# Expanding router gates into a dense matrix: strided evacuations, one-hot blocks of four, and gate products on GpSimd

## The chip, the core and the metric

The kernel runs on one core of one Trainium2 chip. TensorE (PE), VectorE (DVE), ScalarE (ACT), GpSimd (POOL) and SyncE (SP, which here issues transfers) each have a queue of their own, worked off in order, and they wait for one another by semaphores. The metric is device time in microseconds (us) of one execution.

## The reference, cut to what matters

The program is one layer of a streaming encoder for 1152 tokens (1024 prompt, 128 sample tokens): two attention branches, a merge, a product-key mixture of 128 x 128 single-neuron experts (PEER), and a per-layer embedding. The change touches PEER only:

```python
q = (xi @ w_q).reshape(t, PEER_HEADS, 2, PEER_DK // 2)
s = jnp.einsum('thpc,hpnc->thpn', q, sub_keys).astype(jnp.float32)
top_s, top_i = lax.top_k(s, PEER_TOPK)
...
best_s, pos = lax.top_k(cand_s, PEER_TOPK)
idx = jnp.take_along_axis(cand_i, pos, axis=-1)
g = jax.nn.softmax(best_s, axis=-1)
hid = jax.nn.gelu(jnp.einsum('thkd,td->thk', u[idx], xi).astype(jnp.float32))
wgt = (g * hid).astype(xi.dtype)
return jnp.einsum('thk,thkd->td', wgt, v[idx])
```

Every token picks 16 experts in each of 8 heads, 128 in all. An expert has two indices i and j, each below 128 (idx = 128 i + j), and a gate g.

## The kernel before, in words

The nine tiles of 128 tokens are split. For four of them the rows of the chosen experts are gathered one by one (GpSimd indirect transfers, line 813, worked on by DVE in lines 816 and 818). For the five tiles in `DENSE` (640 tokens) all 16384 experts are computed, and a gate that is zero for experts that were not chosen picks out the right ones. Their weights come from a dense matrix G in DRAM, `G_d`, with 128 x 128 gates a token.

Three stages lie one behind the other here.

- `hidden_phase` computes the hidden rows of 36 of the 128 values of j ahead of time. It is planned with low priority, so that it fills gaps in whatever runs; its end reaches into the expansion. In `hidden` the rows of u are split in a high and a low part: `uh` on ACT (line 940) and `ul`, a subtraction, on POOL (line 941; on DVE for rows of the dense phase), then multiplied (line 958) and put through gelu on ACT (line 961).
- `expand_phase` builds G. For each tile, `prepare` turns the index and gate rows (i, j, g, each 128 slots x 128 tokens) so that the slots lie on the partitions: `rb` holds i and j as bf16, `gT` the gates. Then, for each block of W = 8 tokens: DVE compares `iota_i` with the i of each token and gets one-hot rows `oa` in bf16 (line 916), laid out with the eight tokens innermost, and compares `iota` with j to get `ob` in f32 (line 917, called obb in the profile). The product of `oa` with the gate is `ga`, in f32 with 128 contiguous values a token: in every second block (GD = 2) one DVE instruction for all eight tokens (line 919), in the others eight ACT instructions (line 923). Both read `oa` in steps of eight bf16, 16 bytes. PE multiplies ga and ob token by token (line 927) and so sums over the 128 slots: four tokens fill one PSUM bank `pg`. ACT copies a bank into `stage` (line 929). `stage` is [j, token] in SBUF, 64 tokens wide; the copy reads PSUM in order and writes single values in steps of 64 f32. When 64 tokens are there, SP writes `stage` to `G_d` (line 933).
- `dense_phase` then goes over j: it reads the gates of two values of j (line 979), multiplies them with the hidden row (line 987), splits the result, and PE multiplies it with the rows of v (lines 1009 to 1011). The rest of the gathers runs beside it.

Tiles of a pool with tag `oa`, `ga` or `obb` have two buffers each (`ex` has bufs = 2): a block takes over the buffer of the block before the last, when all that read it are done. `pg` comes in turns from two kinds of banks with two buffers each. Order: the order of each queue isn't written by hand. A planner simulates the program with its own model of what instructions cost, and by priorities fixes for each engine the order in which it works.

Of the kernel before, what the change touches and what calls it, by code (L numbers as in the profile page):

```python
# [10 lines left out]
BF = mybir.dt.bfloat16  # L11
# [3 lines left out]
OP = mybir.AluOpType  # L15
# [3 lines left out]
P = 128  # L19
# [16 lines left out]
GD = 2  # L36
# [10 lines left out]
def build(tc, I, O, dbg=None, stop=None):  # L47
    nc = tc.nc
    top = ExitStack()

    def pool(stack, name, bufs=1, **kw):
        return stack.enter_context(tc.tile_pool(name=name, bufs=bufs, reuse_waits="tile", **kw))
# [20 lines left out]
    def bank(name, w=512):  # L73
        return psb.tile([P, 512], F32, tag="b1", name=name)
# [810 lines left out]
    def expand_phase():  # L885

        st = ExitStack()
        ex = pool(st, "ex", 2)
        W = 8
        iota = ex.tile([P, W, P], BF, name="iota", bufs=1)  # L890
        nc.gpsimd.iota(iota, pattern=[[0, W], [1, P]], base=0, channel_multiplier=0, allow_small_or_imprecise_dtypes=True)
        iota_i = ex.tile([P, P, W], BF, name="iota_i", bufs=1)
        nc.gpsimd.iota(iota_i, pattern=[[1, P], [0, W]], base=0, channel_multiplier=0, allow_small_or_imprecise_dtypes=True)
        def prepare(t):
            src = ex.tile([P, 3, P], F32, tag="src", name=f"src{t}")
            nc.sync.dma_start(src, rt_d[t].rearrange("k p c -> p k c"))
            ps = bank(f"rT{t}")
            for k in range(3):
                nc.tensor.transpose(ps[:, k * P:(k + 1) * P], src[:, k, :], ident)
            rb = ex.tile([P, 2, P], BF, tag="rb", name=f"rb{t}")  # L900
            nc.scalar.copy(rb, ps[:, 0:2 * P].rearrange("p (k c) -> p k c", k=2))
            gT = ex.tile([P, P], F32, tag="gT", name=f"gT{t}")
            nc.scalar.copy(gT, ps[:, 2 * P:3 * P])
            return rb, gT

        ready = prepare(DT[0])
        for n, t in enumerate(DT):
            rb, gT = ready
            for c0 in range(0, P, W):
                if c0 % 64 == 0:  # L910
                    stage = ex.tile([P, P, 64], F32, tag="stage", name=f"stage{t}{c0}")
                cw = slice(c0, c0 + W)
                oa = ex.tile([P, P, W], BF, tag="oa", name=f"oa{t}_{c0}")
                ga = ex.tile([P, W, P], F32, tag="ga", name=f"ga{t}_{c0}")
                ob = ex.tile([P, W, P], F32, tag="obb", name=f"obb{t}_{c0}")
                nc.vector.tensor_tensor(oa, iota_i, rb[:, 0, cw].unsqueeze(1).broadcast_to([P, P, W]), op=OP.is_equal)
                nc.vector.tensor_tensor(ob, iota, rb[:, 1, cw].unsqueeze(2).broadcast_to([P, W, P]), op=OP.is_equal)
                if (c0 // W) % GD == 0:
                    nc.vector.tensor_tensor(ga, oa.rearrange("p i c -> p c i"),
                                            gT[:, cw].unsqueeze(2).broadcast_to([P, W, P]), op=OP.mult)  # L920
                else:
                    for c in range(W):
                        nc.scalar.mul(ga[:, c, :], oa[:, :, c], gT[:, c0 + c:c0 + c + 1])  # L923
                for b0 in range(0, W, 4):
                    pg = (bank if b0 % 8 == 0 else zbank)(f"pg{t}{c0}{b0}")
                    for c in range(4):
                        nc.tensor.matmul(pg[:, c * P:(c + 1) * P], ga[:, b0 + c, :], ob[:, b0 + c, :], start=True, stop=True)  # L927
                    o = (c0 + b0) % 64
                    nc.scalar.copy(stage[:, :, o:o + 4].rearrange("p j t -> p t j"), pg.rearrange("p (t j) -> p t j", t=4))
                if c0 == 64 and n + 1 < len(DT):  # L930
                    ready = prepare(DT[n + 1])
                if c0 % 64 == 64 - W:
                    nc.sync.dma_start(G_d[2 * n + c0 // 64], stage)
        st.close()
# [136 lines left out]
    if stop is None or stop == "full":  # L1071
        de = ExitStack()
        hs = ExitStack()
        hp = pool(hs, "hp", 2)
        r2s, res = route_phase(1, B, aT1)
        hidden_phase(hp, *aT1)
        r2s.close()
        expand_phase()
        dp = pool(de, "dp")
        yacc = [dp.tile([P, D], F32, name=f"yacc{t}") for t in DT]  # L1080
        dense_phase(hp, yacc, *aT1)
        gathers(9999)
        sg.close()
        ple_phase(hp, A, DT, yacc, aT1)
        de.close()
        hs.close()
# [104 lines left out]
```

## Time and profile before

| | |
|---|---|
| median of 3 runs (lowest to highest) | 4101.27 us (4084.70 to 4101.39) |
| the profiled execution: its own time | 4085.47 us |
| the span of its trace | 4083.8 us |
| granted TensorE clock in it, mean | 0.964 |
| start of the first oa to the end of the last copy of stage | 2010.8 to 2307.7 us of the span |
| instructions of the expansion: oa, obb, products on DVE | 80, 80, 40 |
| products on ACT, copies of stage on ACT | 320, 160 |

How to read it: a row of a group gives line, engine, operation, the tiles written and read, their shapes, how often, then the busy time, the mean time of one in ns, and the engine's idle time just before them with what ended it. A row of the order of time gives start, duration (both us), engine, line, operation, and in brackets the idle time before it. Instructions of one kind in a row are merged there (x8), and successive instructions of an engine overlap somewhat, so the distance from start to start says what one costs the engine. PE counts each f32 multiplication as two records.

### The profile page before, as it was taken

The numbers are of one execution on the slowest core, as the hardware profiler recorded it, in microseconds if no ns is written. First come the engines' busy times: TensorE is split into PE (matmuls) and PEld (weight loads), VectorE is DVE, ScalarE is ACT, GpSimd is POOL, SyncE is SP. The second block draws the span as 40 slices with busy tenths as digits, with TensorE's granted clock in tenths as the row PEclk, the third lists the DMA queues.
The fourth block names the chain that finished last, engine by engine and source line by source line (L and its number), as shares of the span: only waits on it lengthen the run. The fifth ranks groups of instructions, "written<-read, shape, count | busy, mean of one in ns | idle before, by whom it ended". The sixth has DMA issues, their size and how long they took to land.

```text
span 4083.8 us, 57125 instructions
## 1 busy us (share of the span) xinstructions
PE 3716.3 (91%) x20520; PEld 3048.3 (75%) x20520; DVE 2969.9 (73%) x5571; ACT 1539.4 (38%) x3307; POOL 1721.3 (42%) x1360
## 2 busy tenths in 40 slices
PE   7988899869889897899897899999999999999999
PEld 6555566657767565798886788888888888888876
DVE  5122112899888777799888588888888888888862
ACT  5445412346565411224599722222222222212231
POOL 5112032137767555652310044555555555555520
PEclk8999999879999898899999999999999999999999
DMA  6777733328888898972343589989988998988952
GB/s 206 237 235 208 223 93 124 101 82 268 281 288 275 286 321 294 328 247 88 108 184 165 230 297 314 325 309 315 325 304 304 313 331 316 327 298 311 313 173 71
DMA packets 415116, 1002.49 MB, mean 245 GB/s; under 512 B 38816, under 2 KB 170352, under 8 KB 412400
## 3 DMA queue, kind: packets, MB, share of 16 engines
q0 software_dynamic: 147456, 536.94, 38.0%
q1 hardware_dynamic: 267376, 461.90, 34.0%
q8 instruction: 161, 2.64, 0.3%
q14 instruction: 123, 1.01, 0.1%
HBM read 917.19 MB, written 81.50 MB: 245 GB/s over the span
## 4 chain that ended last, share of the span: by engine, by line
issue 25%; PE 22%; DMA 20%; DVE 19%; POOL 11%; ACT 3%; SPq 0%; POOLq 0%; DVEq 0%; ACTq 0%
DMA v<-in_pv,gi 9%; POOL u L813 6%; DMA u<-in_pu,gi 5%; POOL v L813 4%; DVE gya L818 3%; DVE u L816 3%; PE Sd L547 2%; DMA vs<-in_pv 1%; DMA vcd<-in_vA 1%; PE z L209 1%; PE pu L638 1%; PE hd L958 1%; PE po L497 1%; PE z L210 1%; PE z L211 1%
## 5 line engine op out<-in xcount | busy, mean ns | idle before, releaser
L813 POOL DMA_INDIRECT v<-in_pv,gi x512 | 669.5, 1308 | 794.0 <-DVE gya L818 654.9
L813 POOL DMA_INDIRECT u<-in_pu,gi x512 | 669.2, 1307 | 494.3 <-DVE u L816 374.4
L816 DVE SCALAR_TENSOR_TENSOR u<-u,gn 128x1024 f32<-128x1024 f32 x512 | 630.0, 1239 | 167.0 <-DMA u<-in_pu,gi 164.5
L818 DVE SCALAR_TENSOR_TENSOR gya<-v,hid,gya 128x1024 f32<-128x1024 f32 x512 | 661.1, 1291 | 121.3 <-DMA v<-in_pv,gi 117.4
L1009 PE MATMUL py<-vh,wh 128*128 128x512 f32 x1280 | 507.9, 398 | 46.4 <-DVE yacc L1012 23.0
L1011 PE MATMUL py<-vh,wl 128*128 128x512 f32 x1280 | 497.9, 394 | 6.4 <-DVE wl L941 6.4
L1010 PE MATMUL py<-vl,wh 128*128 128x512 f32 x1280 | 502.4, 394 | 0.2 <-DVE vl L941 0.2
L958 PE MATMUL hd<-aTh,uh 128*128 128x320 f32 x2048 | 483.4, 313 | 21.0 <-ACT gp L961 14.1
L958 PE MATMUL hd<-aTh,ul 128*128 128x320 f32 x2048 | 482.8, 313 | 7.0 <-DVE ul L941 5.7
L958 PE MATMUL hd<-aTl,uh 128*128 128x320 f32 x2048 | 482.0, 313 | 0.0
L958 PEld LDWEIGHTS hd<-aTh,uh 128*128 128x128 f32 x2048 | 351.8, 191 | 31.9 <-ACT gp L961 16.0
L958 PEld LDWEIGHTS hd<-aTh,ul 128*128 128x128 f32 x2048 | 349.9, 190 | 13.7 <-DVE ul L941 7.8
L958 PEld LDWEIGHTS hd<-aTl,uh 128*128 128x128 f32 x2048 | 351.1, 191 | 4.0
L940 ACT CAST vh<-vs 128x1024 fp32r<-128x1024 f32 x128 | 134.1, 1052 | 500.0 <-DMA vs<-in_pv 267.7
L1009 PEld LDWEIGHTS py<-vh,wh 128*128 128x128 f32 x1280 | 242.4, 190 | 106.9 <-DVE yacc L1012 29.4
L1011 PEld LDWEIGHTS py<-vh,wl 128*128 128x128 f32 x1280 | 242.4, 189 | 61.3 <-DVE wl L941 10.6
L1010 PEld LDWEIGHTS py<-vl,wh 128*128 128x128 f32 x1280 | 242.8, 190 | 47.5 <-DVE vl L941 0.4
L940 ACT CAST uh<-us 128x1024 fp32r<-128x1024 f32 x128 | 134.2, 1048 | 285.7 <-PE hd L958 266.7
L940 ACT CAST wh<-ge 128x640 fp32r<-128x640 f32 x128 | 91.9, 727 | 390.7 <-DVE ge L987 195.5
L927 PE MATMUL pg<-obb,ga 128*128 128x128 f32 x1280 | 192.5, 296 | 42.2 <-ACT ga L923 22.2
L927 PEld LDWEIGHTS pg<-obb,ga 128*128 128x128 f32 x1280 | 164.0, 195 | 70.5 <-ACT ga L923 28.8
L1012 DVE TENSOR_TENSOR yacc<-yacc,py 128x1024 f32<-128x1024 f32 x160 | 192.4, 1214 | 11.5 <-PE py L1011 11.5
(1051 smaller groups left out, 7368.7 us busy)
## 6 DMA issues: line engine op xcount, KB each, us to landing
us<-in_uT SPq DMA_DIRECT2D x128, 512.0 KB
vs<-in_pv SPq DMA_DIRECT2D x128, 512.0 KB
G_d<-stage SPq DMA_DIRECT2D x10, 4096.0 KB
gj<-G_d SPq DMA_DIRECT2D x64, 640.0 KB
kcd<-in_kA SPq DMA_DIRECT2D x128, 256.0 KB
vcd<-in_vA SPq DMA_DIRECT2D x128, 256.0 KB
ge_d<-gp SPq DMA_DIRECT2D x36, 320.0 KB
ge<-ge_d SPq DMA_DIRECT2D x36, 320.0 KB
```

The lines of the kernel that those rows point to most:

```text
L209: nc.tensor.matmul(out, lh[:, k, :], wh[:, a:b], start=first and k == 0, stop=False)
L547: nc.tensor.matmul(ps[32 * b4:32 * b4 + 32, :], q3[:, 4 * s + b4, :], rhs, start=br == 1 and q < nch, stop=True)
L813: nc.gpsimd.indirect_dma_start(out=r, out_offset=None, in_=I["pu" if k < P else "pv"], in_offset=bass.IndirectOffsetOnAxis(ap=gi[:, kk:kk ...
L816: nc.vector.scalar_tensor_tensor(r, r, 1.0, n2, op0=OP.mult, op1=OP.mult, accum_out=hid[:, kk:kk + 1])
L818: nc.vector.scalar_tensor_tensor(ya, r, hid[:, kk:kk + 1], ya, op0=OP.mult, op1=OP.add)
L927: nc.tensor.matmul(pg[:, c * P:(c + 1) * P], ga[:, b0 + c, :], ob[:, b0 + c, :], start=True, stop=True)
L940: nc.scalar.copy(out_h, src)
L958: nc.tensor.matmul(ps[sp][:, 0:Nw], a[:, k, :], b[:, k, sp * Nw:(sp + 1) * Nw], start=k == 0 and q == 0, stop=k == 7 and q == 2)
L1009: nc.tensor.matmul(py[:, c], wh[:, ns], vh[:, c], start=a, stop=False)
L1010: nc.tensor.matmul(py[:, c], wh[:, ns], vl[:, c], start=False, stop=False)
L1011: nc.tensor.matmul(py[:, c], wl[:, ns], vh[:, c], start=False, stop=z)
L1012: nc.vector.tensor_tensor(yacc[n], yacc[n], py, op=OP.add)
```

## The change

Four things are changed, all in `expand_phase`.

- `oa` is laid out as two blocks of four tokens, [2, 128, 4] instead of [128, 8], and `iota_i` holds 128 x 4 values, read twice. The comparison is still one DVE instruction of 1024 elements.
- The products in every second block move from DVE (one instruction, eight tokens) to GpSimd (two instructions, four tokens each).
- The products on ACT read `oa` in steps of four bf16, 8 bytes, instead of eight.
- The copy from PSUM swaps its order: for each j it reads the four tokens' values, 128 f32 apart in PSUM, and writes them as a run of four in `stage`.

What is computed, the number of blocks, the work of PE and the transfers stay as they are.

```diff
-        iota_i = ex.tile([P, P, W], BF, name="iota_i", bufs=1)
-        nc.gpsimd.iota(iota_i, pattern=[[1, P], [0, W]], base=0, channel_multiplier=0, allow_small_or_imprecise_dtypes=True)
+        iota_i = ex.tile([P, P, 4], BF, name="iota_i", bufs=1)
+        nc.gpsimd.iota(iota_i, pattern=[[1, P], [0, 4]], base=0, channel_multiplier=0, allow_small_or_imprecise_dtypes=True)
...
-                oa = ex.tile([P, P, W], BF, tag="oa", name=f"oa{t}_{c0}")
+                oa = ex.tile([P, 2, P, 4], BF, tag="oa", name=f"oa{t}_{c0}")
...
-                nc.vector.tensor_tensor(oa, iota_i, rb[:, 0, cw].unsqueeze(1).broadcast_to([P, P, W]), op=OP.is_equal)
+                nc.vector.tensor_tensor(oa, iota_i.unsqueeze(1).broadcast_to([P, 2, P, 4]),
+                                        rb[:, 0, cw].rearrange("p (b c) -> p b c", b=2).unsqueeze(2).broadcast_to([P, 2, P, 4]),
+                                        op=OP.is_equal)
                 nc.vector.tensor_tensor(ob, iota, rb[:, 1, cw].unsqueeze(2).broadcast_to([P, W, P]), op=OP.is_equal)
-                if (c0 // W) % GD == 0:
-                    nc.vector.tensor_tensor(ga, oa.rearrange("p i c -> p c i"),
-                                            gT[:, cw].unsqueeze(2).broadcast_to([P, W, P]), op=OP.mult)
-                else:
-                    for c in range(W):
-                        nc.scalar.mul(ga[:, c, :], oa[:, :, c], gT[:, c0 + c:c0 + c + 1])
+                for b in range(2):
+                    if (c0 // W) % GD == 0:
+                        c = slice(4 * b, 4 * b + 4)
+                        nc.gpsimd.tensor_tensor(ga[:, c, :], oa[:, b, :, :].rearrange("p i c -> p c i"),
+                                                gT[:, c0 + 4 * b:c0 + 4 * b + 4].unsqueeze(2).broadcast_to([P, 4, P]), op=OP.mult)
+                    else:
+                        for c in range(4):
+                            d = c0 + 4 * b + c
+                            nc.scalar.mul(ga[:, 4 * b + c, :], oa[:, b, :, c], gT[:, d:d + 1])
...
-                    nc.scalar.copy(stage[:, :, o:o + 4].rearrange("p j t -> p t j"), pg.rearrange("p (t j) -> p t j", t=4))
+                    nc.scalar.copy(stage[:, :, o:o + 4], pg.rearrange("p (t j) -> p j t", t=4))
```

## The prediction

> **What bounds the kernel now.** I read the busy shares first and then the stretches of the expansion. One pair below means two blocks of eight tokens, one with its gates multiplied on DVE and one on ACT; 640 tokens make 40 pairs.
>
> ```profile
> span 4083.8 us, 57125 instructions
> PE 3716.3 (91%) x20520; PEld 3048.3 (75%) x20520; DVE 2969.9 (73%) x5571; ACT 1539.4 (38%) x3307; POOL 1721.3 (42%) x1360
> ```
>
> ```profile
> core 0: us, PE busy (x) PEld busy (x) DVE busy (x) ACT busy (x) POOL busy (x), PEclk, DMA share, GB/s
> 2010.00:2307.50 297.50, 254.90 (x1706) 226.35 (x1705) 238.59 (x202) 291.31 (x517) 21.69 (x7) 0.97 0.39 158
> 2020.00:2100.00 80.00, 77.23 (x603) 76.03 (x603) 65.68 (x50) 78.90 (x138) 15.87 (x5) 1.00 0.42 162
> 2150.00:2300.00 150.00, 119.79 (x716) 95.05 (x715) 122.31 (x111) 150.00 (x269) 0.00 (x0) 0.99 0.36 151
> ...
> 2400.00:2600.00 200.00, 194.84 (x1035) 172.43 (x1034) 174.28 (x158) 46.11 (x65) 98.95 (x78) 0.99 0.90 310
> ```
>
> Over the whole program PE leads and ACT is the least busy engine. In the expansion (2010 to 2307.5) it is the other way round: ACT is busy for 291 of 297.5 us, and in its second part for 150 of 150. PE is full only in the first part, where hidden rows are mixed in. The last row is the dense phase behind it: PE 195 of 200. So time taken out of the expansion lets a PE-bound phase start earlier by that amount, and nothing there gives it back.
>
> The groups of the stage, and a piece of its order of time on ACT and DVE, say what a pair costs.
>
> ```profile
> L929 ACT COPY stage<-pg 128x512 f32<-128x512 f32 x160 | 153.7, 1154 | 0.7 <-PE pg L927 0.7
> L923 ACT ACTIVATE ga<-oa,gT 128x128 f32<-128x128 bf16 x320 | 138.9, 578 | 0.0
> L917 DVE TENSOR_TENSOR obb<-iota,rb 128x1024 f32<-128x1024 bf16 x80 | 99.8, 1247 | 19.5 <-PE pg L927 19.4
> L919 DVE TENSOR_TENSOR ga<-oa,gT 128x1024 f32<-128x1024 bf16 x40 | 92.8, 2319 | 0.0
> L916 DVE TENSOR_TENSOR oa<-iota_i,rb 128x1024 bf16<-128x1024 bf16 x80 | 54.7, 688 | 34.2 <-ACT ga L923 29.7 <-ACT rb L901 4.4
> ...
> L940 ACT CAST uh<-us 128x1024 fp32r<-128x1024 f32 x9 | 9.4, 1043 | 5.2 <-issue 5.2
> L961 ACT ACTIVATE gp<-hd 128x320 f32<-128x320 f32 x18 | 6.8, 429 | 0.0
> L941 DVE TENSOR_TENSOR ul<-us,uh 128x1024 fp32r<-128x1024 f32 x2 | 2.5, 1226 | 0.5 <-ACT uh L940 0.5
> ```
>
> ```profile
> 2177.99 3.49 ACT L923 ACTIVATE ga<-oa,gT 128x128 f32<-128x128 bf16 x8
> 2181.29 3.78 ACT L929 COPY stage<-pg 128x512 f32<-128x512 f32 x4
> 2184.80 3.48 ACT L923 ACTIVATE ga<-oa,gT 128x128 f32<-128x128 bf16 x8
> ```
>
> ```profile
> 2185.69 2.00 DVE L919 TENSOR_TENSOR ga<-oa,gT 128x1024 f32<-128x1024 bf16 x1
> 2188.31 0.69 DVE L916 TENSOR_TENSOR oa<-iota_i,rb 128x1024 bf16<-128x1024 bf16 x1 [0.62 <-ACT ga L923]
> 2188.92 1.22 DVE L917 TENSOR_TENSOR obb<-iota,rb 128x1024 f32<-128x1024 bf16 x1
> 2190.05 0.68 DVE L916 TENSOR_TENSOR oa<-iota_i,rb 128x1024 bf16<-128x1024 bf16 x1
> ```
>
> From start to start, ACT's eight products take 3.30 us (2177.99 to 2181.29) and its four copies 3.51: 6.81 a pair, 40 x 6.81 = 272, and with uh and gp (9.4 + 6.8) 289 of the 291 seen. ACT's throughput is the length of the stage. DVE needs 0.61 for oa and 1.13 for obb, so 3.48 a pair, and 2.0 for its product.
>
> **The change part by part.** *ACT's copies.* 160 copies keep their elements, but now step through PSUM and write runs of four. Prices of ACT without steps:
>
> ```profile
> 66.69 0.40 ACT L449 ACTIVATE p<-p,sm 128x128 f32<-128x128 f32 x1
> 66.99 0.24 ACT L337 COPY kTs<-tp 128x128 f32<-128x128 f32 x1
> ...
> 3941.33 1.05 ACT L231 CAST aTgh<-n3t1t 128x512 fp32r<-128x512 f32 x2
> 3942.27 1.07 ACT L857 ACTIVATE n<-yacc 128x1024 f32<-128x1024 f32 x1
> ```
>
> Two 128x512 reads of PSUM take 0.94 from start to start, 0.47 each against 0.88 now. No row steps through PSUM on ACT. The ends are 0.47 (only the stepped write cost anything, and four in a row cure it) and, above the present 0.88, 1.29 (the stepped read adds the same 0.41 that the stepped write adds now, on top of it). I take 0.47, the row of the same source, size and type: 1.88 a pair. *ACT's products* read oa at steps of 8 bytes, not 16: between 0.41 as now and 0.30, the row without steps (66.69 to 66.99). I take 0.30: 2.40 a pair. ACT then needs 40 x 4.28 + 19 = 190 us, and 255 with copies as slow as today. Either way it stops being the limit.
>
> [...]
>
> *DVE* loses 40 products of 2.0 us. Its 80 comparisons oa keep 1024 elements in runs of four, not eight. I leave them at 0.61; the upper end is obb's 1.13 (fourth rival); below, nothing in the edit makes them shorter.
>
> *GpSimd* gets 80 products of 128x512, each from bf16 in steps of 8 bytes and a gate that is repeated. The nearest rows are its contiguous f32 operations with two inputs, and one with one input:
>
> ```profile
> L200 POOL TENSOR_TENSOR wo00l<-wo00s,wo00h 128x1024 fp32r<-128x1024 f32 x4 | 9.5, 2384 | 46.1 <-ACT wo00h L199 46.1
> L200 POOL TENSOR_TENSOR wu00l<-wu00s,wu00h 128x768 fp32r<-128x768 f32 x4 | 7.3, 1835 | 0.0
> L141 POOL TENSOR_SCALAR_AFFINE_SELECT t<-t 128x512 f32<-128x512 f32 x4 | 2.5, 641 | 0.0
> ```
>
> Per element (2384 - 1835) / 256 = 2.14 ns; 1835 less 256 x 2.14 gives 1.29 us for 512. Ends: 0.64 (the one-input row) and 2.1, if steps cost POOL what they cost DVE (2.00 against obb's 1.22, a factor 1.64). I take 1.29, since two tensors are still read: 2.58 a pair. [...] A product waits for its oa from DVE and for PE to give back ga; behind it in POOL's queue stand the next product and, in the mixed part, a ul, for which PE's hidden rows wait. The shorter iota_i is made before the stage and costs nothing there.
>
> What matters more is that these products don't run beside DVE:
>
> ```profile
> 2100.03 1.22 DVE L917 TENSOR_TENSOR obb<-iota,rb 128x1024 f32<-128x1024 bf16 x1
> 2101.17 4.13 DVE L919 TENSOR_TENSOR ga<-oa,gT 128x1024 f32<-128x1024 bf16 x1
> ...
> 2100.41 3.11 POOL L941 TENSOR_TENSOR ul<-us,uh 128x1024 fp32r<-128x1024 f32 x1 [12.45 <-ACT uh L940]
> ```
>
> POOL starts at 2100.41, but takes 3.11 and ends at 2103.51, that is 2.26 after obb's end at 2101.25; the DVE product issued at 2101.17 ends at 2105.30, 1.79 after POOL's end. Each waited for the other whole. [...] So DVE and POOL are one resource here: 3.48 + 2.58 = 6.06 a pair, where ACT had 6.81.
>
> *The sum.* The two together need 40 x 6.06 = 242, plus the seven subtractions ul on POOL that the stage holds (7 x 2.26 = 16) and DVE's two (2.5): 261. With about 3 us until the last product has been multiplied and copied out, 264. PE needs at the pace of the mixed stretch 1706 x 77.23 / 603 = 218, so it hides. Against 297 that is 33 us, if the port never idles. It will: DVE waits 19.4 us today for PE to give obb's two buffers back, and that stays; POOL's products queue behind each ul, which waits for ACT's uh (12.45 us above, with nothing behind it today); the waits of DVE for ACT's products (29.7) should mostly go, since those get shorter. I put 17 us on waiting, near the 19.4: stage 281, **16 us less**. The profiled execution took 4085.5 us (span 4083.8): 4069.5, so **4070**. The median of the three runs, 4101.3, is 16 above the profiled one and the lowest, 4084.7, next to it; a median of that upper kind would be 4086. The first gather of the dense phase and the writes of G keep their places behind the stage.
>
> **The rivals.** *POOL's product is cheap.* With bf16 and a repeated gate near the one-input 0.64, the port needs 40 x 4.76 + 19 = 209, PE's 218 is the limit, and with 17 us of waiting the stage is 235: 62 less, 4024. For it: half the bytes on one side. Against it: the slope of 2.14 ns is that of two reads. Chance 0.17.
>
> *POOL's product is dear*, the one that ends slower. At 2.1 us the port needs 40 x (3.48 + 4.2) + 22 = 329, 32 more than the stage has now: 4118. It decides from 1.47 us on, where the port and 17 us of waiting make up 297. For it: the only stepped bf16 product in the trace, L919, pays 64%. Against it: that step is 16 bytes, the new one 8. Chance 0.18.
>
> *The stepped read of PSUM costs what the stepped write did.* At 0.88 ACT needs 255, close to the port's 264, and the two chains wait on each other: some 5 us gained, 4080. At 1.29 it would be 40 x 7.56 + 19 = 321, 24 slower. Chance 0.12, mostly of the first.
>
> *Runs of four slow the comparisons.* At 1.13 each, oa adds 40 x 1.04 = 42 to the port, the stage is 323: 26 slower, 4111. Against it: same bytes, same inner step. Chance 0.08.
>
> **How the numbers follow.** The forecast has 0.45 and by itself spans 4052 (no waiting) to 4085 (waiting eats it all). Half a per cent, 20 us, is about what a measurement of this kernel can tell from no change. The forecast's centre lies just inside that; 0.20 of its 0.45 is beyond. Faster: 0.17 + 0.20 = 0.37. Slower: 0.18, 0.02 from the third and 0.03 from the fourth: 0.23. Within: 0.40. The range goes from 4030, just short of the cheap product's 4024, to 4120, which takes in the dear product and the runs of the upper kind: 4030 to 4120.
>
> **What would show it.** Right: the copies of stage near 0.47 from start to start and the products on ACT near 0.30; ACT no longer full between 2150 and the end of the stage; obb and oa stretched to 2 us and more wherever a POOL product is under way; DVE and POOL busy adding up to about the length of the stage, which ends near 2290; the dense phase as long as before. Wrong: POOL's product clearly off 1.29 us, DVE keeping its 1.22 beside POOL (then the port isn't shared in this form), copies still at 0.88, or a dense phase of another length, since the planner orders all queues anew.

## The result, and the profile after

| | before | after |
|---|---|---|
| median (lowest to highest), 4 runs each | 4097.16 us (4084.70 to 4101.39) | 4034.32 us (4021.52 to 4036.04) |
| the profiled execution: its own time | 4085.47 us | 4036.04 us |
| first oa to the end of the last copy of stage | 2010.8 to 2307.7, 296.9 us | 2017.5 to 2257.4, 239.8 us |
| from there to the end of the span | 1776.1 us | 1776.5 us |

One of the four runs of experiment 1 (4174.46 us, granted clock 0.834) and the only run of experiment 11 (4367.15 us, 0.778) are slow runs, so the first is left out of its median, and of the second only the durations on DVE and POOL are used.

The time after is 0.9845 of that before, interval 0.9814 to 0.9876: 1.5% faster. In the two profiles the expansion is 57.0 us shorter, what lies ahead of it 6.7 us longer, and what lies behind it 0.4 us longer. The sum, 49.9, is the difference of the spans (4083.8 and 4033.9). The 6.7 us say nothing about the change: in the profiles below, two executions of one and the same kernel start the stage at 2015.6 and 2007.5, further apart than that.

The page of the changed kernel, the span and the busy shares:

```profile
span 4033.9 us, 57386 instructions
PE 3674.5 (91%) x20520; PEld 3032.9 (75%) x20520; DVE 2939.1 (73%) x5531; ACT 1446.2 (36%) x3307; POOL 1865.5 (46%) x1440
```

Over the whole program hardly anything moves; the stretches of the changed kernel tell more (busy time of each engine, then granted clock and transfers):

```profile
core 0: us, PE busy (x) PEld busy (x) DVE busy (x) ACT busy (x) POOL busy (x), PEclk, DMA share, GB/s
2017.00:2257.50 240.50, 213.96 (x1695) 208.53 (x1694) 209.01 (x162) 199.50 (x517) 159.00 (x87) 0.99 0.49 195
2060.00:2100.00 40.00, 40.00 (x325) 40.00 (x324) 39.04 (x28) 34.30 (x90) 29.21 (x17) 1.00 0.48 190
2165.00:2257.00 92.00, 67.82 (x532) 63.18 (x532) 71.49 (x63) 76.38 (x200) 54.55 (x32) 0.98 0.44 188
2350.00:2550.00 200.00, 194.21 (x1041) 172.85 (x1041) 176.04 (x160) 45.97 (x65) 108.75 (x79) 1.00 0.92 316
```

ACT did 517 instructions in the stage before and does 517 now, but in 200 us, not 291, and it is no longer full in the second part (76 of 92 us). In the first part, where the nine hidden rows are mixed in, PE is now full: 40.00 of 40.00. The dense phase looks as it did (PE 194 of 200).

The groups of the stage in the changed kernel (busy time, mean ns of one, idle time just before them and what ended it):

```profile
L924 POOL TENSOR_TENSOR ga<-oa,gT 128x512 f32<-128x512 bf16 x80 | 140.8, 1779 | 81.7 <-PE pg L933 65.6 <-DVE oa L917 11.5 <-DVE obb L920 2.3
L920 DVE TENSOR_TENSOR obb<-iota,rb 128x1024 f32<-128x1024 bf16 x80 | 118.2, 1500 | 7.6 <-PE pg L933 7.6
L929 ACT ACTIVATE ga<-oa,gT 128x128 f32<-128x128 bf16 x320 | 100.8, 401 | 5.2 <-DVE oa L917 5.2
L917 DVE TENSOR_TENSOR oa<-iota_i,rb 128x1024 bf16<-128x1024 bf16 x80 | 93.1, 1188 | 23.9 <-POOL ga L924 19.7 <-ACT rb L902 4.1
L935 ACT COPY stage<-pg 128x512 f32<-128x512 f32 x160 | 88.9, 581 | 33.7 <-PE pg L933 33.1
```

The copies' mean falls from 1154 to 581 ns, and that of ACT's products from 578 to 401. ACT now waits 33.1 us for PE, where it waited 0.7. DVE's comparisons have become *longer* in the mean: obb from 1247 to 1500 ns, oa from 688 to 1188. The order of time of the changed kernel in the second part shows why (start, duration, engine; in brackets the idle time before):

```profile
2225.81 1.17 ACT L935 COPY stage<-pg 128x512 f32<-128x512 f32 x2
2226.40 1.23 DVE L920 TENSOR_TENSOR obb<-iota,rb 128x1024 f32<-128x1024 bf16 x1 [0.28 <-PE pg L933]
2226.44 3.54 POOL L924 TENSOR_TENSOR ga<-oa,gT 128x512 f32<-128x512 bf16 x2 [2.19 <-PE pg L933]
...
2227.54 1.53 DVE L917 TENSOR_TENSOR oa<-iota_i,rb 128x1024 bf16<-128x1024 bf16 x1
...
2229.11 2.51 ACT L929 ACTIVATE ga<-oa,gT 128x128 f32<-128x128 bf16 x8 [0.20 <-DVE oa L917]
2230.01 0.69 DVE L917 TENSOR_TENSOR oa<-iota_i,rb 128x1024 bf16<-128x1024 bf16 x1 [0.94 <-POOL ga L924]
...
2230.62 1.22 DVE L920 TENSOR_TENSOR obb<-iota,rb 128x1024 f32<-128x1024 bf16 x1
...
2232.12 1.23 DVE L920 TENSOR_TENSOR obb<-iota,rb 128x1024 f32<-128x1024 bf16 x1 [0.28 <-PE pg L933]
2232.16 2.08 POOL L924 TENSOR_TENSOR ga<-oa,gT 128x512 f32<-128x512 bf16 x1 [2.19 <-PE pg L933]
```

From 2226.40 to 2232.12, 5.72 us, is one pair. POOL is issued at 2226.44, while obb runs, and its two products end at 2229.98. In between DVE's oa, which takes 0.69 alone, lasts 1.53. The order fits one holder at a time. obb ends at 2227.63. POOL's first product ends 2.08 after its issue, as the last row shows for the next pair, so at 2228.52: 0.89 after obb's end. oa ends at 2229.07, 0.55 later, and POOL's second product at 2229.98, another 0.91. Then oa and obb run undisturbed. Only 0.31 us of the pair (0.03 and 0.28) lie between instructions of the two. So a POOL product holds DVE up for some 0.9 us; below I use 0.91. The last seven pairs of the stage all look like this one. The six ahead of them, in another order of DVE's queue, take 5.18 to 5.35; there DVE idles only while POOL works (0.93 before the oa at 2179.95 and again at 2185.30), and 5.35 is DVE's own 3.48 and two products of some 0.93. Over the last 14 pairs of the stage, from the start of the 51st oa to that of the 79th, the mean is 5.62.

### The profile page after: what moved, and what is told of

It reads as the page before. It is cut to its first block, busy times and chain, and to the rows that moved or that the text cites. A ratio compares the mean times of both kernels' runs of the same rounds, so it can differ in the third digit from the quotient of the medians.

```text
span 4033.9 us, 57386 instructions
## 1 busy us (share of the span) xinstructions
PE 3674.5 (91%) x20520; PEld 3032.9 (75%) x20520; DVE 2939.1 (73%) x5531; ACT 1446.2 (36%) x3307; POOL 1865.5 (46%) x1440
## 4 chain that ended last, share of the span: by engine, by line
PE 30%; DVE 19%; DMA 19%; issue 18%; POOL 12%; ACT 2%; SPq 0%; POOLq 0%; DVEq 0%; ACTq 0%
DMA v<-in_pv,gi 7%; POOL u L813 6%; DMA u<-in_pu,gi 6%; PE hd L964 5%; POOL v L813 3%; DVE gya L818 3%; DVE u L816 3%; PE pg L933 3%; PE Sd L547 2%; PE py L1015 2%; PE py L1017 2%; PE py L1016 2%; PE pu L638 1%; DMA vs<-in_pv 1%; PE z L209 1%
## 5 line engine op out<-in xcount | busy, mean ns | idle before, releaser
L813 POOL DMA_INDIRECT v<-in_pv,gi x512 | 680.3, 1329 | 582.8 <-DVE gya L818 451.2
L497 PE MATMUL po<-pT,vU 128*64 128x128 f32 x1056 | 153.0, 290 | 34.6 <-ACT pT L80 34.0
L933 PE MATMUL pg<-obb,ga 128*128 128x128 f32 x1280 | 158.8, 279 | 26.5 <-POOL ga L924 19.5
```

The lines of the kernel that those rows point to most:

```text
L497: nc.tensor.matmul(po[64 * h:64 * h + 64, 0:P], vU[:, k0 + j, 64 * h:64 * h + 64], pT[:, j, :], start=j == 0, stop=j == nk - 1)
L813: nc.gpsimd.indirect_dma_start(out=r, out_offset=None, in_=I["pu" if k < P else "pv"], in_offset=bass.IndirectOffsetOnAxis(ap=gi[:, kk:kk ...
```

## The experiments

My theory after the result: ACT set the length of the stage, the copies alone bring most of the gain, and DVE and POOL take turns, so that the move to GpSimd brings nothing by itself. The rivals: the move is needed, because DVE with its product would be the next limit; or the stretched comparisons have another cause than reads on POOL. "Pair" means the same two blocks as in the prediction, in the second part, where no hidden rows are mixed in; the time given is that of most pairs there, and where two kernels are close, the mean of the last 14 pairs stands beside it.

**1. The copies alone.** Before, with only the new copy:

```diff
-                    nc.scalar.copy(stage[:, :, o:o + 4].rearrange("p j t -> p t j"), pg.rearrange("p (t j) -> p t j", t=4))
+                    nc.scalar.copy(stage[:, :, o:o + 4], pg.rearrange("p (t j) -> p j t", t=4))
```

> The kernel before with one line of the change, the copies that step through PSUM and write runs of four. The stage took 296.9 us before (first oa to the end of the last copy of stage) and 239.9 in the changed kernel. Theory (ACT was the limit, and its copies were the larger part of its relief): ACT falls from 6.81 to 3.30 + 1.88 = 5.18 us a pair, DVE with its own product needs 3.48 + 1.95 = 5.43 and becomes the limit; 40 x 5.43 = 217, with 16 for POOL's seven ul, 3 for DVE's two, 3 for the tail and some 10 of waiting a stage of about 250: 47 less, a time of 0.988 to 0.990 of the kernel before. Rival (DVE's products had to leave DVE): DVE's waits for ACT and PE stay and eat most of it, stage 275 or longer.

Measured: 4044.49 us (median of three runs), ratio 0.9876 (0.9843 to 0.9909); stage 252.9 us, 44.0 of the 57.0. The order of time of DVE and of ACT in this kernel:

```profile
2219.38 2.01 DVE L919 TENSOR_TENSOR ga<-oa,gT 128x1024 f32<-128x1024 bf16 x1
2221.27 0.72 DVE L916 TENSOR_TENSOR oa<-iota_i,rb 128x1024 bf16<-128x1024 bf16 x1
2221.87 1.25 DVE L917 TENSOR_TENSOR obb<-iota,rb 128x1024 f32<-128x1024 bf16 x1
2223.01 0.72 DVE L916 TENSOR_TENSOR oa<-iota_i,rb 128x1024 bf16<-128x1024 bf16 x1
2223.61 1.25 DVE L917 TENSOR_TENSOR obb<-iota,rb 128x1024 f32<-128x1024 bf16 x1
2224.74 2.02 DVE L919 TENSOR_TENSOR ga<-oa,gT 128x1024 f32<-128x1024 bf16 x1
```

```profile
2222.07 3.47 ACT L923 ACTIVATE ga<-oa,gT 128x128 f32<-128x128 bf16 x8
2225.43 2.03 ACT L929 COPY stage<-pg 128x512 f32<-128x512 f32 x4
```

No row has a bracket. DVE doesn't wait here, at 5.36 us a pair (2219.38 to 2224.74); its product costs 1.89 from start to start. But ACT doesn't wait either: eight products and the four copies behind them take 5.33 (from 2222.07 to the next product at 2227.40), and ACT is busy for 114.87 of the 115 us from 2155 to 2270, DVE for 111.15. Which of the two sets the pair, this run doesn't decide; both are near their limit. Over the last 14 pairs the mean is 5.38, where the changed kernel, with GpSimd at work, needs 5.62.

**2. The blocks of four alone.** The changed kernel with the products back on DVE and the old copies (both edits are those of experiments 3 and 4).

> The changed kernel with its products on DVE instead of GpSimd, and with the old copies: of the change only the one-hot rows in blocks of four are left. Theory: ACT stays the limit with 3.51 + 2.40 = 5.91 us a pair, 40 x 5.91 + 19 = 255, stage about 260. DVE's product, two instructions of 512 at steps of 8 bytes: if it is the 16-byte step that made 1024 elements take 2.0 instead of 1.22, they take about 0.7 each, otherwise 1.0 each. Rival (the products' steps don't matter, what helped was the copies and POOL): products on ACT stay at 0.41 and the stage at 290.

Measured: 4056.08 us in one run; stage 262.3, pairs of 5.88. DVE's product for four tokens costs 0.60 from start to start, 1.20 for a block, against 1.89: a smaller step makes DVE's own product a third cheaper. ACT is the limit again: 8 x 0.30 + 4 x 0.87 = 5.88.

**3. Everything but GpSimd.** The changed kernel with the products back on DVE:

```diff
-                        nc.gpsimd.tensor_tensor(ga[:, c, :], oa[:, b, :, :].rearrange("p i c -> p c i"),
+                        nc.vector.tensor_tensor(ga[:, c, :], oa[:, b, :, :].rearrange("p i c -> p c i"),
```

> The changed kernel with the products of every second block on DVE (two instructions of four tokens) instead of GpSimd; all else as changed. Theory (DVE and POOL are one resource, so moving a product from DVE to POOL saves nothing by itself, and the blocks of four would have made it cheap on DVE): DVE needs 3.48 + 1.2 = 4.7 us a pair where DVE and POOL together now take 5.72; the second part of the stage, where no hidden rows are mixed in, shrinks to about 4.8 a pair, the stage to 215 to 225 against 239.9. Rival (POOL takes work off DVE): DVE alone with 3.48 + 2.0 and ACT's order make pairs of 5.8 or more, stage 245 to 260.

Measured: 4021.30 us, ratio 0.9816 (0.9783 to 0.9849); stage 229.8, 10 us *shorter* than with GpSimd. It missed the expected 215 to 225, on the theory's side. DVE's order of time in it, and two of its stretches:

```profile
2218.23 1.29 DVE L924 TENSOR_TENSOR ga<-oa,gT 128x512 f32<-128x512 bf16 x2
2219.44 0.69 DVE L917 TENSOR_TENSOR oa<-iota_i,rb 128x1024 bf16<-128x1024 bf16 x1
...
2221.78 1.22 DVE L920 TENSOR_TENSOR obb<-iota,rb 128x1024 f32<-128x1024 bf16 x1
2222.91 1.29 DVE L924 TENSOR_TENSOR ga<-oa,gT 128x512 f32<-128x512 bf16 x2
```

```profile
core 0: us, PE busy (x) PEld busy (x) DVE busy (x) ACT busy (x) POOL busy (x), PEclk, DMA share, GB/s
2015.00:2245.50 230.50, 223.56 (x1712) 216.81 (x1711) 203.89 (x242) 196.53 (x517) 17.64 (x7) 0.99 0.51 203
2155.00:2245.00 90.00, 84.49 (x624) 78.82 (x623) 84.98 (x109) 84.03 (x230) 0.00 (x0) 1.00 0.50 211
```

A pair takes 4.68 us (2218.23 to 2222.91), DVE's 3.48 and 1.20 without a gap. In the first part a pair takes 6.63 in the mean, since PE is full there (43.00 of 43.00 us from 2017 to 2060); that is why the stage didn't shrink by 40 x 1.04. PE is busy for 223.6 of 230.5 us: this version is nearly at what PE needs.

**4. Everything but the copies.** The changed kernel with the old copy line (the diff of experiment 1, reversed).

> The changed kernel with the old copies (PSUM read in order, single values written 256 bytes apart); products on GpSimd and blocks of four as changed. Theory: ACT is the limit again with 3.51 + 2.40 = 5.91 us a pair against the 5.72 of DVE and POOL, and the two chains disturb each other: stage 255 to 265, so the copies are worth 15 to 25 us on top of the rest. Rival (the copies carry the whole gain): stage back above 285.

Measured: 4054.45 us in one run; stage 256.8, pairs of 5.88. ACT's two groups in it:

```profile
L935 ACT COPY stage<-pg 128x512 f32<-128x512 f32 x160 | 153.7, 1124 | 1.4 <-PE pg L933 1.4
L929 ACT ACTIVATE ga<-oa,gT 128x128 f32<-128x128 bf16 x320 | 101.6, 441 | 0.0
```

ACT waits 1.4 us in the whole stage: it is the limit, as in experiment 2, and the pair is the same 5.88, whichever engine makes the other products.

**5. GpSimd with the old layout.** Before, with the new copies and the products on GpSimd, reading `oa` in steps of 16 bytes:

```diff
+                    for b in range(2):
+                        c = slice(4 * b, 4 * b + 4)
+                        nc.gpsimd.tensor_tensor(ga[:, c, :], oa[:, :, c].rearrange("p i c -> p c i"),
+                                                gT[:, c0 + 4 * b:c0 + 4 * b + 4].unsqueeze(2).broadcast_to([P, 4, P]), op=OP.mult)
```

> The kernel before with the new copies and with the products of every second block on GpSimd (two instructions of four tokens), but one-hot rows still in blocks of eight, so that GpSimd and ACT read them in steps of 16 bytes. Theory: a step of 16 bytes costs GpSimd something like the 64% that it costs DVE (2.00 against 1.22): a product takes 1.5 us or more undisturbed instead of 1.04, DVE and POOL together 3.48 + 2 x 1.4 = 6.3 a pair, stage about 265 against 239.9. Rival (GpSimd doesn't care for the step): pairs of 5.7 as in the changed kernel, stage 240 to 245; ACT with 3.30 + 1.88 = 5.18 hides in both.

Measured: 4050.87 us in one run; stage 256.1, between the two. The shortest product takes 1.27 us, against 1.04 in the changed kernel: the step costs POOL 22%, not the 64% that I had carried over from DVE. Most of its pairs in the second part take 5.64, which lies between the changed kernel's 5.35 and 5.72; over the last 14 pairs the means are 5.68 and 5.62.

The seven kernels so far make a table of the stage's length, in us:

| | products on DVE | products on GpSimd |
|---|---|---|
| old layout, old copies | 296.9 (before) | not run |
| old layout, new copies | 252.9 | 256.1 |
| blocks of four, old copies | 262.3 | 256.8 |
| blocks of four, new copies | 229.8 | 239.8 (after) |

With the old copies GpSimd saves 5.5 us; with the new ones it costs 3 or 10. The two other edits bring the whole gain. Each entry is from one profile; for the two kernels of the last row a second one (experiments 9 and 10) is within 0.5 us. Where the 5.5 us come from no run here shows: the pair of the second part is the same.

**6 and 7. Is it the reading?** In the changed kernel one more GpSimd instruction a pair, whose result nothing uses: in one kernel a product that reads two tiles, in the other a memset, which reads nothing.

```diff
+        junk = ex.tile([P, 4, P], F32, name="junk", bufs=1)
...
+                if (c0 // W) % GD == 1:
+                    nc.gpsimd.tensor_tensor(junk, iota[:, 0:4, :], iota[:, 4:8, :], op=OP.mult)
```

```diff
+        junk = ex.tile([P, 4, P], F32, name="junk", bufs=1)
...
+                if (c0 // W) % GD == 1:
+                    nc.gpsimd.memset(junk, 0.0)
```

> The changed kernel with one more GpSimd instruction a pair that nobody needs: a product of two bf16 tiles in SBUF, 128x512, into a scratch tile. Theory (DVE's instructions with two inputs and GpSimd's exclude each other): though GpSimd idles for 2.2 us of each pair of 5.72, the pair gets longer by about the instruction's 0.9, stage 20 to 36 longer than 239.9. Rival (what limits is the chain oa, product, PE and the two buffers, not a shared resource): the instruction falls into GpSimd's idle time and the stage stays within 5 us.

> As the run before, but the additional GpSimd instruction fills the scratch tile with zeros and reads nothing. Theory (what is shared is the read side): it hides, the stage stays within 5 us of 239.9. Rival (GpSimd excludes DVE whatever it does, or its queue is the limit): the stage gets longer by 40 times its duration, as with the reading one.

Measured: stage 285.8 us with the product (4081.99 us in all), 46.0 more than in the changed kernel, and 248.6 with the memset (4037.98), 8.8 more. Both are more than expected. But nothing held these instructions back, and the planner ran all of them ahead, in the first part, where POOL also has the ul to make for which PE's hidden rows wait. So part of the 46 and 8.8 us may have come by POOL's queue, and the two theories aren't told apart. Experiments 11 and 12 mend that.

**8. What a GpSimd product costs, by form.** In the changed kernel, 21 products of 128x512 behind the last block, whose results nothing uses, in seven forms:

```diff
...
+        forms = (("fa", ga[:, 0:4, :], ob[:, 0:4, :]), ("fb", iota[:, 0:4, :], ob[:, 0:4, :]), ("fc", s8, ob[:, 0:4, :]),
+                 ("fd", s8, bc), ("fe", s16, bc), ("ff", ga[:, 0:4, :], bc), ("fg", iota[:, 0:4, :], bc))
+        for q in range(3):
+            for nm, x, y in forms:
+                j = ex.tile([P, 4, P], F32, tag="junk", name=f"{nm}{q}", bufs=2)
+                nc.gpsimd.tensor_tensor(j, x, y, op=OP.mult)
```

Here s8 and s16 are bf16 in steps of 8 and of 16 bytes, and bc is the gate, one value repeated for 128 elements.

> The changed kernel with 21 GpSimd products of 128x512 behind the last block, three each of seven forms: both f32 in order; bf16 and f32 in order; bf16 in steps of 8 bytes and f32 in order; the form of the change (bf16 in steps of 8 bytes, repeated gate); bf16 in steps of 16 bytes and a repeated gate; f32 in order and a repeated gate; bf16 in order and a repeated gate. It asks why the product took 1.04 us undisturbed and not the 1.29 that the f32 rows gave. If the repeated gate saves the second read, every form with it is near 1.0 and the others near 1.29; if bf16 does, the forms with bf16 are; if neither, 1.29 was wrong for f32 as well. A step of 16 bytes shows its price as the fifth form against the fourth.

POOL's order of time in it, one round of the forms (fa to fg):

```profile
2255.24 1.28 POOL L948 TENSOR_TENSOR fa<-ga,obb 128x512 f32<-128x512 f32 x1 [1.21 <-ACT ga L929]
2256.47 1.16 POOL L948 TENSOR_TENSOR fb<-iota,obb 128x512 f32<-128x512 bf16 x1
2257.59 1.31 POOL L948 TENSOR_TENSOR fc<-oa,obb 128x512 f32<-128x512 bf16 x1
2258.86 1.05 POOL L948 TENSOR_TENSOR fd<-oa,gT 128x512 f32<-128x512 bf16 x1
2259.86 1.28 POOL L948 TENSOR_TENSOR fe<-iota,gT 128x512 f32<-128x512 bf16 x1
2261.09 1.05 POOL L948 TENSOR_TENSOR ff<-ga,gT 128x512 f32<-128x512 f32 x1
2262.09 1.05 POOL L948 TENSOR_TENSOR fg<-iota,gT 128x512 f32<-128x512 bf16 x1
```

Two whole f32 tensors take 1.28, just the 1.29 of the prediction's slope. Put the repeated gate in place of one of them (ff) and it is 1.05. With the gate, f32 or bf16 makes no difference (ff and fg, 1.05 both), nor does the step of 8 bytes (fd, the form of the change, 1.05); the step of 16 bytes costs 0.23 (fe, 1.28), that is 22%. Beside a whole second operand the step of 8 bytes isn't free: 1.31 against 1.16 (fc, fb). In the two other rounds all rows are within 0.03 us of these but two (fd 2.03, fb 2.16), which ran beside a subtraction on DVE; DVE's rows of the changed kernel have two, of 1.23 us each, in this stretch, at 2264.61 and 2271.65.

**9 and 10. GpSimd or DVE, measured closer.** The changed kernel unaltered, and the kernel of experiment 3, side by side in five rounds.

> The changed kernel unaltered, timed beside the run after it on the same chip. All theories: as before, 0.981 to 0.988 of the kernel before, stage 240.

> The changed kernel with its products on DVE instead of GpSimd, once more and beside the changed one. Theory (the stage is 10 us shorter with DVE, 229.8 against 239.9, and the rest takes as long): 10 us or 0.25% faster than the changed kernel in the medians. Rival (the difference of 13 us between the earlier medians is the scatter of the runs): the two within 4 us.

Measured: 4035.59 us, ratio 0.9846 (0.9821 to 0.9871), and 4026.07 us, ratio 0.9840 (0.9819 to 0.9862). The stages are 239.9 and 230.2 us, as before. The medians are 9.5 us apart in the expected direction, but the intervals of the ratios overlap. So the 10 us in the stage are shown, twice; that the whole time is shorter by as much is likely and not shown by the times alone.

**11 and 12. Reading or only writing, held in place.** As 6 and 7, but the extra instruction writes a third part of `ga` of every second block (ACT's blocks) that nothing multiplies, so that it has to wait for that buffer:

```diff
-                ga = ex.tile([P, W, P], F32, tag="ga", name=f"ga{t}_{c0}")
+                ga = ex.tile([P, W + 4, P], F32, tag="ga", name=f"ga{t}_{c0}")
...
+                if (c0 // W) % GD == 1:
+                    nc.gpsimd.tensor_tensor(ga[:, W:W + 4, :], iota[:, 0:4, :], iota[:, 4:8, :], op=OP.mult)
```

(in 12, `nc.gpsimd.memset(ga[:, W:W + 4, :], 0.0)`).

> The changed kernel with one more GpSimd instruction a pair that nobody needs, a product of two bf16 tiles, 128x512. Unlike in the earlier run it writes into a third part of ga in the blocks that ACT multiplies, so that it can't run ahead: it waits for ga's buffer like the rest. Theory (DVE's and GpSimd's reads exclude each other): pairs of the second part, 5.72 before, become 6.4 to 6.8; the stage 25 to 40 longer than 239.9. Rival (GpSimd's idle time takes it): pairs of 5.7 to 5.9.

> As the run before, but the additional instruction fills the same part of ga with zeros (0.53 us in the earlier run) and reads nothing. Theory (only reads are shared): pairs of 5.7 to 5.9 and a stage within 10 of 239.9. Rival (GpSimd holds DVE off whatever it does, or its queue is in the way): pairs longer by 0.5 and the stage by 20.

With the memset: 4036.42 us, stage 239.3. POOL's order of time in it:

```profile
2219.64 0.52 POOL L931 MEMSET ga<- 128x512 f32 x1
2221.88 3.53 POOL L924 TENSOR_TENSOR ga<-oa,gT 128x512 f32<-128x512 bf16 x2 [1.73 <-PE pg L935]
2225.35 0.52 POOL L931 MEMSET ga<- 128x512 f32 x1
2227.60 3.52 POOL L924 TENSOR_TENSOR ga<-oa,gT 128x512 f32<-128x512 bf16 x2 [1.73 <-PE pg L935]
2231.07 0.52 POOL L931 MEMSET ga<- 128x512 f32 x1
```

A memset takes its 0.52 beside DVE's oa too (the one at 2225.35, with an oa from 2225.44 that keeps its 0.69); all 40 take 0.522 in the mean, and a pair stays at 5.72 (2225.35 to 2231.07). The pairs of 5.35, in which the shared resource has no gap to hide it, stay at 5.35 too (oa at 2180.76 and 2186.10); the mean of the last 14 is 5.52. With the product the time is 4367.15 and the stage 281.9, not to be set beside the others; the durations on DVE and POOL are, since a short oa takes 0.68 and the median copy 0.585 in both kernels. Rows of DVE and POOL from its order of time:

```profile
2402.78 3.19 DVE L920 TENSOR_TENSOR obb<-iota,rb 128x1024 f32<-128x1024 bf16 x2
2403.00 3.88 POOL L924 TENSOR_TENSOR ga<-oa,gT 128x512 f32<-128x512 bf16 x2 [0.69 <-DVE oa L917]
...
2405.90 3.09 DVE L917 TENSOR_TENSOR oa<-iota_i,rb 128x1024 bf16<-128x1024 bf16 x2
2406.84 1.59 POOL L931 TENSOR_TENSOR ga<-iota 128x512 f32<-128x512 bf16 x1
```

DVE has no idle time left: a pair is 6.13 (the next obb starts at 2408.91), which is DVE's own 3.48 and three products of 0.88. Where a pair took 5.72, the 0.31 us that were free are filled first, so it grew by 0.41, less than the 0.7 to 1.1 expected; against the pairs of 5.35 it is 0.78. The mean of the last 14 goes to 6.13, from 5.62. So in these pairs an added GpSimd instruction that reads takes time from DVE (6.13 in the place of 5.72), and one that only writes takes none (5.72).

## Why the prediction was right and wrong

**The limit and what hides the rest: right.** ACT set the stage: with the old copies a pair takes 5.88 in two kernels that differ in the engine of the other products. The copies went to 0.47 from start to start and the products to 0.30, the values taken. The stepped read of PSUM costs nothing that shows: 0.47 is also the price of the contiguous read that the prediction took it from (third rival out). The dense phase gave nothing back: 1776.1 and 1776.5 us behind the stage.

**One resource out of DVE and POOL: right.** It shows in the pairs of the second part, and experiments 11 and 12 separate it from other causes. No run shows the port that the prediction's sums name; what the runs showed in its place is that DVE's comparisons and the POOL instructions that read take turns, a POOL product holding DVE up for 0.91 us, while the memset, which only writes, left the pair at 5.72. oa kept its 0.61 from start to start (2230.01 to 2230.62; fourth rival out). But the sign that I named for it was wrong: DVE's and POOL's busy times don't add up to the stage (209 and 159 in 240.5), since each one's waiting for the other counts as busy. The stretched instructions were the better sign: 1500 ns for obb and 1188 for oa in the mean, though the typical oa beside POOL took 1.53 us and not the 2 us named.

**The step that failed: the price of POOL's product**, "I take 1.29, since two tensors are still read". The stage lost 57 us and not 16, and this term is most of the difference. The slope was that of two whole tensors, and for those it holds (fa 1.28). The gate is one value repeated for 128 elements, and that form takes 1.05 (fd); beside DVE it holds it up for 0.91. So the prediction's reason to choose 1.29 fell with the very part of the operand that its text named ("a gate that is repeated"). Of the 0.38 between 1.29 and 0.91, 0.24 is the form of the operand; the other 0.14 is that the sum took a product's whole duration as time in which DVE is held up. In the sum that is 80 x 0.38 = 30 us: 40 x (3.48 + 1.82) = 212 in the place of 242.

**The second mis-sized term: 17 us of waiting.** With the corrected price, and the 16, 2.5 and 3 us as they stood, the sum is 234; the stage took 239.8, which leaves about 6 for waiting. DVE's wait for PE's obb buffers, expected to stay at 19.4, fell to 7.6. Its 19.7 us of waiting for POOL (oa <- POOL ga) cost nothing of their own: POOL was holding the shared resource in that time (0.94 at 2230.01). The two terms, 30 and 11, are the 41 us between the 281 forecast and the 240 measured. PE being full in the first part means that the 6 are a remainder and not a measured wait. One rival was summed otherwise: the 329 of the dear product leaves out the 17 us of waiting that the forecast and the cheap rival carry.

**The cheap rival came nearest**, with 235 for the stage, but by another road: it had 0.64 for the product and PE as the limit. PE is the limit in the first part only.

**What the prediction didn't ask:** whether the move was worth making. Its own terms gave 6.06 for DVE with POOL and 5.48 for DVE with its old product (3.48 + 2.0). The last 14 pairs say 5.62 (5.68 in the old layout) and 5.38, and 4.68 once DVE, too, reads in steps of 8 bytes.

The version with the shortest stage in these runs is that of experiment 3: the new copies and the blocks of four, with the products on DVE.

## What to carry to other kernels

When an edit has several parts, price each with the others undone: here two parts bring the whole gain and the third takes some of it back, which the total of 1.5% doesn't show. Before work is moved from VectorE to GpSimd, look for a place in the trace where both read at once. Here they took turns, and with both other edits made the move cost 10 us of the stage (239.8 against 229.8): for four tokens a GpSimd product held VectorE up for 0.91 us, where VectorE's own cost 0.60, and VectorE's had got cheaper by its better step (1.20 a block against 1.89). Take an operation's price from a row with the same form of operands, a repeated one among them, and not only of the same number: here 1.05 against 1.28.

## What the runs showed of the hardware

- Writing single f32 values 256 bytes apart cost ACT 0.88 us from start to start for 128x512 (kernel before), runs of four 0.47 (changed kernel), as much as contiguous (two in 0.94 at 3941.33 of the kernel before), although the new copies read PSUM in steps of 512 bytes.
- In the products of these runs a step of 16 bytes in the bf16 operand cost more than one of 8 on each of three engines, but not by the same factor: DVE 1.89 against 1.20 us for 1024 elements (in one and in two instructions; experiments 1 and 3), ACT 0.41 against 0.30 for 128 (before, after), POOL 1.28 against 1.05 for 512 (fe, fd of experiment 8). At 8 bytes POOL paid nothing beside a repeated operand (fd and fg, 1.05 both); beside a whole one it was 1.31 against 1.16 (fc, fb).
- On POOL a second operand that is one value repeated saved 0.23 of 1.28 us beside f32 in order (fa, ff) and 0.11 of 1.16 beside bf16 in order (fb, fg).
- A POOL product that waits for DVE shows as busy: 1.78 us in the mean of the 80 in the changed kernel, 1.05 alone (fd).
